# Row sums of reciprocals: a new hand-written order in which GpSimd squares most of the pairs and TensorE folds four rows

## The chip, the cores and the metric

The kernel runs on one core of a Trainium2 chip. The metric is the device time of one execution in microseconds (us). The core has five engines that run their own instruction lists side by side: TensorE (PE in the profile), VectorE (DVE), ScalarE (ACT), GpSimd (POOL) and SyncE (SP), which here issues every load and store. Sixteen DMA engines move the data.

## The reference

```python
x = abs(randn(32, 512, 1024)) + 1e-6      # float32
out = np.sum(1.0 / x, axis=-1)            # float32, shape (32, 512)
```

So 16384 rows of 1024 numbers are read, 67.1 MB, and one sum of reciprocals is written for each.

## The kernel before, in words

The 16384 rows are laid on 128 partitions with 128 rows each. What the kernel calls "row r" is therefore a 128x1024 tile, one row on each partition, 512 KB in memory. Rows 0 to 127 are loaded in order into a ring of 46 places (`ring`, `R = 46`), so row r lies in place r mod 46 and can be loaded only when everything that reads row r - 46 is done. The sums go to the 128 columns of `sums`, which is stored at the end.

No engine divides. A row is turned into sums of 1/x in one of two ways.

**Alone.** ScalarE replaces x by 1/sqrt(x) in place (token `A`, line 178; one instruction may take several neighbouring rows, written `A3+2`). Then the squares are summed, in one of four ways:

- `Z` (line 187): ScalarE squares the row and accumulates the sum.
- `G` (line 280), then `T` (line 283): GpSimd squares the row in place, VectorE adds it up.
- `Q` (line 240): VectorE multiplies the row by itself and accumulates, in one instruction with two inputs from the ring.
- `B` (line 255): VectorE takes batch-norm statistics of the two halves. The sums of squares lie in small tiles of counts, means and variances. Near the end of a block of such rows, `K` (line 265, ScalarE) squares the means and `M` (line 270, VectorE) adds them to the variances for all rows of the block at once. `C` is a plain square on ScalarE without a sum, for `T` to add.

**As a pair.** With a and b the two halves of a row, 1/a + 1/b = (a + b) / (a b). GpSimd multiplies the halves into one of five slots of `prod` (`P`, line 194). TensorE adds the halves in a bank of PSUM through an identity matrix (`U`, line 201, two matmuls). ScalarE takes 1/sqrt of the product in its slot (`L`) and squares it (`E`; both line 211). VectorE multiplies that by the sum in PSUM and accumulates (`R`, line 220). A pair row needs no `A`, and each of its later instructions works on 512 columns.

The order of all of this is one hand-written list, `PLAN`. Each engine executes its tokens in the order of the list, and a token waits only for the data it touches. `D` issues a load of so many rows from SyncE (line 170), `O` the stores of the finished columns (line 156); a last store of the remaining columns follows after the list. In the list before there are 25 loads: 2, 12, 12, 9 and 11 rows fill the ring, then 10, 8, 8, 8 and so on, down to four of one row. The last row, 127, comes as two halves (`PIECES`), which count as units 127 and 128. It ends:

```python
... A122 R119 A123 Q122 L121 Q123 A124 E121 Q124 A125
R121 A126 Q125 A127 A128 Q127 Z126 Q128
```

Of the kernel before, what the change touches and what calls it, by code (L numbers as in the profile page):

```python
# [11 lines left out]
def kernel(  # L12
# [17 lines left out]
    STATS = ((43, 3, 11), (80, 2, 18),)  # L30
    STORES = (0, 21, 43, 64, 81, 99, 116)
    S = float(2**17)
    FIT = 1.0 - 2.0**-17

    PLAN = """
        D2 D12 D12 D9 D11 A0+2 Z0 A2 A3 A4+3 G1+3 A7 A8 A9 G6+3 A10 T1 A11+3 T2+2 Z4 Z5 G9 Z10
        Z12 G11 T6+4 D10 A14 A15+2 G13 A17+3 G16 T11 T13 A20+4 G17 Q15 G19 T16+2 A24+2 G20 A26
        A27 G21 A28+2 G23+3 A30+2 T19+3 A32+3 Z14 D8 G26 C33 Z18 G27 Z22 Z29 G28 A35+2 G30+3
        T23+6 D8 A37+3 A40+4 G34+2 T30+2 A44+2 Z36 T32 G40 Z37 T33+3 D8 Z38 G44+2 U53@0 A46+2
        T40 A48 Q42 G47 A49 A50+3 B43 T44 P53@0 T45 A54+2 G50 B46 L53 T47 Z39 D6 B49 A56+6 T50
        B52 Q54 B55 A62+2 G57 Q56 E53 G60 Z41 D6 R53 Z48 T57 A64+6 B58 G62 T60 G63 B61 T62+2
        A70+2 G65+2 B64 Z51 D7 D6 B67 Z59 D5 G68+2 A72 T65+2 D4 A73+4 B70 G71+2 T68+2 D3 A77+2
        B73 A79 G78 T71+2 D2 K0 U81@1 A80 A82+2 G79 M0 B80 A84 U85@2 B82 P81@1 Z74 D2 T78+2 Z75
        G83 L81 Z76 D2 P85@2 B84 U89@3 A86+3 T83 P89@3 U91@4 P91@4 L85 B86 G87 L89 A90 B88 L91  # L50
        T87 E81 E85 E89 R81 E91 R85 Z77 D1 D1 D1 D1 D1 D1 R89 B90 A92+2 P95@0 U95@5 R91 A94 B92
        G93 L95 B94 A96 A97 T93 A98 B96 E95 B98 Z97 P99@1 U99@6 A100+2 R95 P103@2 L99 B100 G101
        A102 U103@7 L103 B102 A104 T101 E99 E103 R99 P107@3 U107@0 A105 R103 A106 B104 P109@4
        U109@1 L107 Q105 A108 L109 B106 E107 E109 R107 P111@0 U111@2 A110 B108 A112 P113@1 R109
        U113@3 L111 B110 L113 E111 B112 E113 P115@2 U115@4 A114 R111 P116@3 L115 R113 U116@5
        E115 B114 P118@4 A117 R115 U118@6 L116 K1 Q117 L118 E116 P119@0 M1 O0 A120 U119@7 R116
        E118 Q120 L119 E119 P121@1 U121@0 R118 A122 R119 A123 Q122 L121 Q123 A124 E121 Q124 A125
        R121 A126 Q125 A127 A128 Q127 Z126 Q128
# [3 lines left out]
    Square = mybir.ActivationFunctionType.Square  # L62
    mult = mybir.AluOpType.mult
    add = mybir.AluOpType.add
# [18 lines left out]
    ring = pool.tile([P, R, D], f32)  # L83
    sums = pool.tile([P, F], f32)
    prod = pool.tile([P, NP, H], f32)
    stat_rows = [i for lo, step, n in STATS for i in range(lo, lo + step * n, step)]
    stats = pool.tile([P, len(stat_rows), 2, 2, 3], f32)
# [9 lines left out]
    def place(u):  # L97
        return (u, 0, D) if u < NR else PIECES[u - NR]

    def area(u, n=1):  # L100
        r, at, w = place(u)
        if u >= NR:
            w, n = sum(place(i)[2] for i in range(u, u + n)), 1
        return ring[:, r % R : r % R + n, at : at + w]
# [35 lines left out]

    def rows(u, n=1):
        spaces = []
        for r, at, w in (place(i) for i in range(u, u + n)):
            spaces += [("row", r % R, i) for i in range(at, at + w, 128)]
        return spaces

    def half(u, at):
        return [("row", u % R, i) for i in range(at, at + H, 128)]

    loaded = 0  # L150
    summed = set()
    slot, bank = {}, {}
# [5 lines left out]
    with tc.manual_schedule():  # L158
        for _ in range(EARLY):
            nc.gpsimd.nop(hint="idle", nofuse=True)  # L160
        for op, u, n, b in (parse(tok) for tok in PLAN):
            if op == "D":
                n, u = u, loaded
                while n:
                    r, at, w = place(u)
                    m = min(n, R - r % R, NR - u, HALF - r % HALF) if u < NR else n
                    k = m
                    if u >= NR:
                        w, k = sum(place(i)[2] for i in range(u, u + m)), 1
                    inst = nc.sync.dma_start(  # L170
                        out=area(u, m),
                        in_=x_v[r // HALF, :, r % HALF : r % HALF + k, at : at + w],
                    )
                    note("SP", inst, writes=rows(u, m))
                    u, n = u + m, n - m
                loaded = u
# [8 lines left out]
            elif op == "Z":  # L185
                r = place(u)[0]
                inst = nc.scalar.activation(  # L187
                    out=area(u), in_=area(u), func=Square, accum_out=sums[:, r : r + 1]
                )
                summed.add(r)  # L190
                note("ACT", inst, writes=rows(u))
# [6 lines left out]
            elif op == "U":  # L198
                bank[u], r = b, u % R
                for h in range(2):  # L200
                    inst = nc.tensor.matmul(  # L201
                        ps[:, b],
                        lhsT=ident,
                        rhs=ring[:, r, h * H : (h + 1) * H],
                        start=h == 0,
                        stop=h == 1,
                    )
                    note("PE", inst, half(u, h * H), [("bank", b)])
            elif op in "LE":
# [8 lines left out]
            elif op == "R":  # L218
# [9 lines left out]
                    accum_out=sums[:, u : u + 1],  # L228
                )
                note("DVE", inst, [("bank", bank[u])], [("slot", slot[u])])  # L230
            elif op == "Q":
                r, at, w = place(u)
                joined = [u]
                while len(joined) < n:
                    joined += [i for i in range(NR, u) if place(i)[0] == r][-len(joined) :][:1]
                at -= sum(place(i)[2] for i in joined[1:])
                w += sum(place(i)[2] for i in joined[1:])
                row = ring[:, r % R, at : at + w]
                total = sums[:, r : r + 1]
                inst = nc.vector.tensor_tensor_reduce(  # L240
                    out=row,
                    in0=row,
                    in1=row,
                    scale=1.0,
                    scalar=total if r in summed else 0.0,
                    op0=mult,
                    op1=add,
                    accum_out=total,
                )
                summed.add(r)  # L250
                note("DVE", inst, writes=[s for i in joined for s in rows(i)])
            elif op == "B":
                i = stat_rows.index(u)
                for h in range(2):
                    inst = nc.vector.bn_stats(  # L255
                        out=stats[:, i, h], in_=ring[:, u % R, h * H : (h + 1) * H]
                    )
                    note("DVE", inst, reads=half(u, h * H), writes=[("stat", i)])
            elif op in "KM":
                lo, step, n = STATS[u]  # L260
                i = stat_rows.index(lo)
                part = stats[:, i : i + n]
                if op == "K":
                    mean = part[:, :, :, :, 1].rearrange("p f h e -> p (f h e)")
                    inst = nc.scalar.activation(  # L265
                        out=mean, in_=mean, func=Square, scale=float(H // 2) ** 0.5
                    )
                    engine = "ACT"
                else:
                    inst = nc.vector.tensor_reduce(  # L270
                        out=sums[:, lo : lo + step * (n - 1) + 1 : step],
                        in_=part[:, :, :, :, 1:].rearrange("p f h e k -> p f (h e) k"),
                        axis=mybir.AxisListType.XY,
                        op=add,
                    )
                    engine = "DVE"
                note(engine, inst, writes=[("stat", j) for j in range(i, i + n)])
            elif op == "G":
                row = area(u, n)
                inst = nc.gpsimd.tensor_tensor(out=row, in0=row, in1=row, op=mult)  # L280
                note("POOL", inst, writes=rows(u, n))
            elif op == "T":
                inst = nc.vector.tensor_reduce(  # L283
                    out=sums[:, u : u + n],
                    in_=area(u, n),
                    axis=mybir.AxisListType.X,
                    op=add,
                )
                note("DVE", inst, reads=rows(u, n))
# [34 lines left out]
```

## Time and profile before

| | |
|---|---|
| median of 3 runs | 166.06 us (166.04 to 166.06) |
| span of the profiled execution | 164.2 us; the runs count some 1.8 us more, which lie around the span |
| busy: ScalarE, VectorE, GpSimd | 145.7, 115.9, 108.8 us |
| busy: TensorE matmuls | 38.2 us |
| read from memory | 67.11 MB, 409 GB/s over the span |

The page has numbered parts: busy time of each engine, the span in 40 slices with a digit for each engine's busy share, the DMA queues, the chain of work that ended last, the costliest groups of instructions, and the DMA issues. "L178" is line 178 of the kernel. In a group, "mean ns" is the duration of one instruction; two instructions that follow each other on an engine can overlap at their ends, so the distance from one start to the next start is a little shorter. `SPq` is the queue in which SyncE issues DMAs.

### The profile page before, as it was taken

How to read it: one execution, taken by the hardware profiler on the slowest of the kernel's cores; microseconds unless marked ns; L12 is line 12 of the kernel's file. 1: busy time of each engine (PE TensorE's matmuls, PEld its weight loads, DVE VectorE, ACT ScalarE, POOL GpSimd, SP SyncE). 2: the span in 40 equal slices, each digit the busy share in tenths (PEclk: the TensorE clock that was granted, in tenths of full speed). 3: DMA queues.
4: the chain of work that ended last, by engine and by line, in shares of the span. 5: the costliest groups of instructions: out<-in, count | busy, mean ns of one | idle time of the engine just before them, and what ended most of it. 6: DMA issues, size and time to landing. Idle time of an engine off the chain costs nothing.

```text
span 164.2 us, 640 instructions
## 1 busy us (share of the span) xinstructions
PE 38.2 (23%) x68; PEld 14.4 (9%) x68; DVE 115.9 (71%) x147; ACT 145.7 (89%) x148; POOL 108.8 (66%) x56
## 2 busy tenths in 40 slices
PE   0000000000000000053000000065908198699700
PEld 0000000000000000020000000032302033234200
DVE  0000003559927039999999999999698969999894
ACT  3600199999999999999999999999999999999994
POOL 1000069998999999999507979999926195477300
PEclk9999999999999999999999999999975859999985
DMA  5999899899989899999998998999999999999970
GB/s 188 463 539 407 383 395 563 383 431 431 463 351 527 351 479 409 391 455 431 391 503 383 431 463 381 455 407 441 419 425 467 414 419 422 421 411 417 408 249 2
DMA packets 4611, 67.20 MB, mean 409 GB/s; under 512 B 1408, under 2 KB 1408, under 8 KB 2176
## 3 DMA queue, kind: packets, MB, share of 16 engines
q1 hardware_dynamic: 4608, 67.18, 96.3%
q14 instruction: 3, 0.02, 0.0%
HBM read 67.11 MB, written 0.07 MB: 409 GB/s over the span
## 4 chain that ended last, share of the span: by engine, by line
ACT 63%; DMA 26%; DVE 6%; issue 2%; POOL 2%; SPq 0%; DVEq 0%; POOLq 0%
ACT ring L178 47%; DMA ring<-in_x_dram 26%; ACT ring L187 10%; ACT prod L211 6%; DVE ring L240 2%; DVE stats L255 2%; POOL prod L194 2%; DVE prod L220 1%; DVE sums L283 0%; SPq L170 0%; ACT stats L265 0%; DVE sums L240 0%; DVE sums L220 0%; DVEq L240 0%; POOLq L194 0%
## 5 line engine op out<-in xcount | busy, mean ns | idle before, releaser
L178 ACT ACTIVATE ring<-ring 128x1024 f32<-128x1024 f32 (+4 forms) x65 | 104.1, 1658 | 15.2 <-DMA ring<-in_x_dram 15.1
L280 POOL TENSOR_TENSOR ring<-ring 128x1024 f32<-128x1024 f32 (+2 forms) x33 | 85.9, 2634 | 29.9 <-ACT ring L178 29.9
L283 DVE TENSOR_REDUCE sums<-ring 128x1 f32<-128x1024 f32 (+4 forms) x27 | 53.3, 1999 | 42.2 <-POOL ring L280 42.1
L201 PE MATMUL ps<-ring,ident 128*128 128x512 f32 x68 | 38.2, 712 | 117.2 <-DMA ring<-in_x_dram 115.9
L255 DVE BATCH_NORM_STATS2 stats<-ring 128x6 f32<-128x512 f32 x58 | 36.5, 679 | 3.1 <-ACT ring L178 3.1
L194 POOL TENSOR_TENSOR prod<-ring 128x512 f32<-128x512 f32 x17 | 22.5, 1339 | 15.0 <-DMA ring<-in_x_dram 10.8
L201 PEld LDWEIGHTS ps<-ring,ident 128*128 128x128 f32 x68 | 14.4, 224 | 140.2 <-POOL ring L280 71.6
L187 ACT ACTIVATE ring<-ring 128x1024 f32<-128x1024 f32 x23 | 23.9, 1041 | 0.0
L211 ACT ACTIVATE prod<-prod 128x512 f32<-128x512 f32 x34 | 19.8, 615 | 0.2
L240 DVE CUSTOM_DVE_ANT_0 ring<-ring 128x1024 f32<-128x1024 f32 (+1 forms) x12 | 17.6, 1480 | 0.5 <-ACT ring L178 0.4
L220 DVE CUSTOM_DVE_ANT_0 prod<-prod,ps 128x512 f32<-128x512 f32 x17 | 11.1, 676 | 0.1
L187 ACT ACTIVATION_READ_ACCUMULATOR ring<-ring 128x1 f32 x23 | 4.3, 187 | 0.0
L70 ACT ACT_TABLE_LOAD x1 | 1.3, 1283 | 0.7 <-PEq L308 0.7
L220 DVE DVE_READ_ACCUMULATOR2_ANT sums<- 128x1 f32 x17 | 1.4, 81 | 0.0
L240 DVE DVE_READ_ACCUMULATOR2_ANT sums<- 128x1 f32 x13 | 1.0, 81 | 0.0
L240 DVE CUSTOM_DVE_ANT_0 ring<-ring,sums 128x512 f32<-128x512 f32 x1 | 0.8, 752 | 0.1
masks.py:199 POOL TENSOR_SCALAR_AFFINE_SELECT ident<-ident 128x128 f32<-128x128 f32 x1 | 0.3, 293 | 0.5 <-POOL ident masks.py:197 0.5
L265 ACT ACTIVATE stats<-stats 128x44 f32<-128x44 f32 (+1 forms) x2 | 0.5, 272 | 0.0
L270 DVE TENSOR_REDUCE sums<-stats 128x11 f32<-128x88 f32 (+1 forms) x2 | 0.5, 264 | 0.0
masks.py:197 POOL MEMSET ident<- 128x128 f32 x1 | 0.2, 205 | 0.3 <-POOLq L308 0.3
L308 POOL MEMSET const-float32-0.0<- 128x1 f32 x1 | 0.1, 99 | 0.2 <-issue 0.2
L308 POOL MEMSET const-bfloat16-1.0<- 128x1 bf16 x1 | 0.1, 102 | 0.0
(2 smaller groups left out, 0.2 us busy)
## 6 DMA issues: line engine op xcount, KB each, us to landing
ring<-in_x_dram SPq DMA_DIRECT2D x2, 6144.0 KB, 25.8
ring<-in_x_dram SPq DMA_DIRECT2D x3, 4096.0 KB, 26.0
ring<-in_x_dram SPq DMA_DIRECT2D x3, 3072.0 KB, 26.3
ring<-in_x_dram SPq DMA_DIRECT2D x1, 5632.0 KB, 55.9
ring<-in_x_dram SPq DMA_DIRECT2D x1, 5120.0 KB, 32.4
ring<-in_x_dram SPq DMA_DIRECT2D x1, 4608.0 KB, 43.3
ring<-in_x_dram SPq DMA_DIRECT2D x4, 1024.0 KB, 37.8
ring<-in_x_dram SPq DMA_DIRECT2D x1, 3584.0 KB, 24.4
```

The lines of the kernel that those rows point to most:

```text
L70: nc.scalar.add_instruction(mybir.InstLoadActFuncSet(name=nc.get_next_instruction_name(), act_func_set_id=act_sets.index("abs_reciprocal_s ...
L178: inst = nc.scalar.activation(out=area(u, n), in_=area(u, n), func=Arsqrt if op == "A" else Square, scale=FIT if op == "A" else 1.0,)
L187: inst = nc.scalar.activation(out=area(u), in_=area(u), func=Square, accum_out=sums[:, r : r + 1])
L194: inst = nc.gpsimd.tensor_tensor(out=prod[:, b], in0=ring[:, r, :H], in1=ring[:, r, H:], op=mult)
L201: inst = nc.tensor.matmul(ps[:, b], lhsT=ident, rhs=ring[:, r, h * H : (h + 1) * H], start=h == 0, stop=h == 1,)
L211: inst = nc.scalar.activation(out=pair, in_=pair, func=Arsqrt if op == "L" else Square, scale=S * FIT if op == "L" else 1.0,)
L220: inst = nc.vector.tensor_tensor_reduce(out=pair, in0=pair, in1=ps[:, bank[u]], scale=S, scalar=0.0, op0=mult, op1=add, accum_out=sums[:, ...
L240: inst = nc.vector.tensor_tensor_reduce(out=row, in0=row, in1=row, scale=1.0, scalar=total if r in summed else 0.0, op0=mult, op1=add, acc ...
L255: inst = nc.vector.bn_stats(out=stats[:, i, h], in_=ring[:, u % R, h * H : (h + 1) * H])
L265: inst = nc.scalar.activation(out=mean, in_=mean, func=Square, scale=float(H // 2) ** 0.5)
L280: inst = nc.gpsimd.tensor_tensor(out=row, in0=row, in1=row, op=mult)
L283: inst = nc.vector.tensor_reduce(out=sums[:, u : u + n], in_=area(u, n), axis=mybir.AxisListType.X, op=add,)
```

## The change

The list is new, and so are some of its tokens.

- 18 of 21 pairs are now squared by GpSimd (`H`, in place in the slot) instead of by ScalarE (`E`, which stays for rows 39, 119 and 122). Before there were 17 pairs, all squared by ScalarE.
- Four rows (44, 45, 85, 86), after GpSimd has squared them, are folded by TensorE: `V44+2` adds the quarters of two rows into one PSUM bank by four matmuls, and `F44+2` on VectorE reduces the 2x256 columns there. This stands in for a `T` over two rows.
- `stats` now has a place for each of rows 0 to 121 and is zeroed by GpSimd at the start. Every sum of these rows, whatever made it, is written into one cell of it, and two `K`/`M` pairs (rows 0 to 77, rows 78 to 121) turn all of them into `sums`. Only rows 122 to 127 write `sums` themselves.
- Rows 125, 126 and 127 are counted in quarters of 256 columns (units 125 to 136). 23 loads bring everything: 17, 13 and 16 rows fill the ring, then 10, 8, 12, 9, 7, 7, 6, 5, 4, 3, 2, 2, 2, 1, 1 rows, rows 125 and 126, and row 127 as two quarters and a half.
- 13 idle instructions at the start of GpSimd's list are gone.
- By kinds, before and after: rows through `A` 111 and 107; `Z` 23 and 17; rows through `G` 46 and 31; rows through `T` 47 and 34; `B` 29 and 46; `Q` 13 and 6; `C` 1 row and 7; pairs 17 and 21.

```diff
-    EARLY = 13
...
-    PIECES = ((127, 0, 512), (127, 512, 512))
-    NR = 127
-    STATS = ((43, 3, 11), (80, 2, 18),)
-    STORES = (0, 21, 43, 64, 81, 99, 116)
+    NR = 125
+    C = D // 4
+    BLOCKS = (78, 122,)
+    STORES = (0, 9, 18, 27, 37, 46, 55, 64, 78)
...
+        D17 D13 D16 A8 A5+3 C5 A0+4 A14 G0 A4 Z1 G8 B4 A9+4 T5 G14 B7 T8 G2 A16 B12 Z11 G10
+        U26@0 T2 A29 T14 Z3 P27@0 B29 A23 G9 U27@1 A25 L27 T9+2 Z23 H27 A17+4 G16 T0 P26@1
+        B6 B25 D10 A21+2 G17 T16 A15 R27 C21 L26 C15 H26 A13 R26 T15 A24 C24 T21 A28 B19 G28
+        T17 A45 U34@2 A35+4 B20 P34@2 T24 P39@3 T28 G45 B13 A30+3 B18 G37 D8 B22 A40 A42+2
+        D12 G40 A41 T40 B41 A50 P51@4 U51@3 T37 A46 G43 L34 C42 U39@4 G31+2 C50 A44 T50 A47
+        T42+2 L51 H34 L39 E39 H51 C38 B30 G44 A52+4 T31 R51 U60@5 G36 B46 A48+2 P56@0 T36
+        V44+2@6 B35 P60@1 A57+2 B53 G49 A33 T38 G47 U56@7 Z54 T32 Z33 F44+2 R34 L60 D9 A61+3
...
+        P103@2 B97 L98 Z100 U98@4 H98 B99 A104 P102@3 U103@5 L101 Q104 L103 L102 R98 U101@6
+        A107+2 D4 P105@4 F85+2 B94 P106@0 U102@7 L105 B108 A109 H101 Z109 U105@0 B107 H102
+        L106 H103 R101 A110+3 D4 U113@1 B96 H105 R103 P113@1 U106@2 R102 Z110 B112 H106 D1
+        L113 U114@3 P114@2 R105 A115+2 B111 H113 R106 L114 D1 P118@3 U118@4 R113 A117 B115
+        H114 Z116 B117 A120 D2 O0 P119@4 U119@5 R114 L118 B120 L119 H118 E119 U122@6 A121
+        P122@0 R119 R118 K1 A123 Q121 L122 Q123 E122 A124 R122 A125+4 Q124 A129+4 Q125+4
+        A133+2 A135+2 Q129+4 Z133+4 M1
...
-        for _ in range(EARLY):
-            nc.gpsimd.nop(hint="idle", nofuse=True)
+        note("POOL", nc.gpsimd.memset(stats, 0.0), writes=result(0, BLOCKS[-1]))
...
+            elif op == "H":
+                pair = prod[:, slot[u]]
+                inst = nc.gpsimd.tensor_tensor(out=pair, in0=pair, in1=pair, op=mult)
+                note("POOL", inst, writes=[("slot", slot[u])])
+            elif op == "V":
+                bank[u] = b
+                w = H // n
+                for h in range(2 * n):
+                    inst = nc.tensor.matmul(
+                        ps[:, b].rearrange("p (n w) -> p n w", n=n),
+                        lhsT=ident,
+                        rhs=whole(u, n)[:, :, h * w : (h + 1) * w],
+                        start=h == 0,
+                        stop=h == 2 * n - 1,
+                    )
+                    note("PE", inst, rows(u, n), [("bank", b)])
+            elif op == "F":
+                inst = nc.vector.tensor_reduce(
+                    out=total(u, n),
+                    in_=ps[:, bank[u]].rearrange("p (n w) -> p n w", n=n),
+                    axis=mybir.AxisListType.X,
+                    op=add,
+                )
+                note("DVE", inst, [("bank", bank[u])], result(u, n))
```

More of the change, by code (lines that the diff above doesn't have):

```diff
@@ L275 @@
                     )
-                    engine = "DVE"
-                note(engine, inst, writes=[("stat", j) for j in range(i, i + n)])
+                    note("DVE", inst, means + result(lo, hi - lo))
             elif op == "G":
@@ L283 @@
                 inst = nc.vector.tensor_reduce(
-                    out=sums[:, u : u + n],
-                    in_=area(u, n),
+                    out=total(u, n),
+                    in_=whole(u, n),
                     axis=mybir.AxisListType.X,
```

141 lines of the change are left out of this document (68 added, 73 removed).

## The prediction

> **What bounds the kernel now.** I read the page from its head to the chain of work that ended last.
>
> ```profile
> span 164.2 us, 640 instructions
> ...
> ACT  3600199999999999999999999999999999999994
> ...
> q1 hardware_dynamic: 4608, 67.18, 96.3%
> q14 instruction: 3, 0.02, 0.0%
> ...
> ACT 63%; DMA 26%; DVE 6%; issue 2%; POOL 2%; SPq 0%; DVEq 0%; POOLq 0%
> ```
>
> Two things are full at once. The load queue's packets fill 96.3% of the span, 158.1 of 164.2 us, so 128 rows cost 1.235 us each and the stream hardly pauses. ScalarE is at 9 in every slice from about 20 us to the end. So two views matter next: when the stream ends (the table by stages), and what stands behind it (the timelines of ScalarE and VectorE at the end).
>
> ```profile
> 140.00:150.00 10.00, 8.69 (x21) 3.51 (x20) 10.00 (x23) 9.87 (x15) 6.26 (x5) 1.00 1.00 420
> ...
> 159.00:160.00 1.00, 0.00 (x0) 0.00 (x0) 1.00 (x3) 1.00 (x2) 0.00 (x0) 0.50 0.21 24
> ```
> ```profile
> 157.79 3.03 ACT L178 ACTIVATE ring<-ring 128x1024 f32<-128x1024 f32 x4
> 160.73 1.04 ACT L187 ACTIVATE ring<-ring 128x1024 f32<-128x1024 f32 x1
> 161.67 0.19 ACT L187 ACTIVATION_READ_ACCUMULATOR ring<-ring 128x1 f32 x1
> ```
> ```profile
> 161.18 0.75 DVE L240 CUSTOM_DVE_ANT_0 ring<-ring,sums 128x512 f32<-128x512 f32 x1
> 161.85 0.08 DVE L240 DVE_READ_ACCUMULATOR2_ANT sums<- 128x1 f32 x1
> ```
>
> The last columns are DMA share and GB/s, ahead of them come PE, PEld, DVE, ACT and POOL. From 140 to 150 us the DMA share is 1.00 with DVE and ACT full too. Between 159 and 160 us the stream runs out: a share of 0.21, 24 GB/s. ScalarE ends at 161.86, VectorE at 161.93, some 2 us behind the last data; the last store and the end take the remaining 2.3 us to 164.2. The runs shown (median 166.06) lie 1.8 us above that span; I carry both 2.3 and 1.8 over unchanged.
>
> So a faster kernel must shorten either the stream or what ScalarE and VectorE still have to do when the last rows arrive. ScalarE work saved in the middle is worth nothing by itself.
>
> **Part 1: what is removed, added and moved, by engine.** Durations, busy and mean ns:
>
> ```profile
> L255 DVE BATCH_NORM_STATS2 stats<-ring 128x6 f32<-128x512 f32 x58 | 36.5, 679 | 3.1 <-ACT ring L178 3.1
> L178 ACT ACTIVATE ring<-ring 128x1024 f32<-128x1024 f32 x36 | 36.4, 1041 | 11.6 <-DMA ring<-in_x_dram 11.6
> L178 ACT ACTIVATE ring<-ring 128x2048 f32<-128x2048 f32 x15 | 28.3, 1895 | 3.6 <-DMA ring<-in_x_dram 3.5
> L187 ACT ACTIVATE ring<-ring 128x1024 f32<-128x1024 f32 x23 | 23.9, 1041 | 0.0
> L194 POOL TENSOR_TENSOR prod<-ring 128x512 f32<-128x512 f32 x17 | 22.5, 1339 | 15.0 <-DMA ring<-in_x_dram 10.8 <-DVE stats L255 2.4 <-DVE sums L283 1.7
> L280 POOL TENSOR_TENSOR ring<-ring 128x3072 f32<-128x3072 f32 x4 | 21.2, 5306 | 20.3 <-ACT ring L178 20.3
> L211 ACT ACTIVATE prod<-prod 128x512 f32<-128x512 f32 x34 | 19.8, 615 | 0.2
> L178 ACT ACTIVATE ring<-ring 128x3072 f32<-128x3072 f32 x7 | 19.2, 2747 | 0.0
> L283 DVE TENSOR_REDUCE sums<-ring 128x1 f32<-128x1024 f32 x15 | 17.9, 1206 | 27.4 <-POOL ring L280 27.4
> L280 POOL TENSOR_TENSOR ring<-ring 128x2048 f32<-128x2048 f32 x5 | 17.9, 3601 | 0.9 <-ACT ring L178 0.9
> L220 DVE CUSTOM_DVE_ANT_0 prod<-prod,ps 128x512 f32<-128x512 f32 x17 | 11.1, 676 | 0.1
> L270 DVE TENSOR_REDUCE sums<-stats 128x18 f32<-128x144 f32 x1 | 0.3, 293 | 0.0
> L270 DVE TENSOR_REDUCE sums<-stats 128x11 f32<-128x88 f32 x1 | 0.2, 235 | 0.0
> ```
> ```profile
> 155.81 0.61 ACT L211 ACTIVATE prod<-prod 128x512 f32<-128x512 f32 x1
> 156.33 1.04 ACT L178 ACTIVATE ring<-ring 128x1024 f32<-128x1024 f32 x1
> 157.27 0.61 ACT L211 ACTIVATE prod<-prod 128x512 f32<-128x512 f32 x1
> ```
> ```profile
> 156.14 1.22 DVE L240 CUSTOM_DVE_ANT_0 ring<-ring 128x1024 f32<-128x1024 f32 x1
> ```
> ```profile
> 5.48 1.91 ACT L178 ACTIVATE ring<-ring 128x2048 f32<-128x2048 f32 x1 [3.46 <-DMA ring<-in_x_dram]
> ```
>
> Starts show what one costs in a full queue: a 512-column activation 0.52 us, a row 0.945; two and three rows in one instruction 1.80 and 2.65 (their means less the same 0.095); a `Z` 1.04 (0.945 and the read of its sum). VectorE by the same reduction (0.07 to 0.08): a `B` row 1.20, `R` 0.605, `T` 1.12, a `Q` near the end 1.15.
>
> - ScalarE: `L` and `E` fall from 34 to 24 (-5.2 us), `Z` from 23 to 17 (-6.2), rows through `A` from 111 to 107 (-3.4 at 0.85 for a row inside a larger instruction), `C` adds 6 (+5.4). Together some -9.5 us. But its work now begins with the first load of 17 rows, near 24 us (3 us to the first bytes and 17 rows) instead of 5.5 us for two rows and 20 us for the rest. It gains room in the middle only.
> - VectorE: 17 more `B` rows (+20.4), 13 fewer rows through `T` (about -14.5), 7 fewer `Q` (about -8.5), 4 more `R` (+2.4), 2 `F` over 512 PSUM columns (taken at an `R`, 0.6 each): about +1.
> - GpSimd: 15 fewer rows through `G` (-26 at 1.7), 4 more `P` (+5.4), 18 `H` (below) and the memset. No row shows a memset of this size; it lies under the first load, which covers it for over 20 us, so I take nothing for it, between a gain of nothing (the 13 idle instructions ran there too) and a delay that only these 20 us would use up.
> - TensorE: 16 more matmuls, none that an engine on the path waits for.
>
> **H has no row.** It is a square of 512 columns in place. The nearest rows are `G`, the same form on 2048 columns (3.60 us for two rows, 5.31 for three, so 1.71 for one more row), and `P`, 512 columns with two different inputs. `G`'s slope carries 512 columns to 0.85 plus a fixed 0.19: 1.04 us. Ends: 0.85 (slope alone) and 1.34 (`P`'s mean). I take 1.04, because `H` has the form of `G`: one operand, read twice, written in place.
> The Trainium skill (GPSIMD Engine Reference, section 3.1) gives a two-input elementwise operation about 2.6 cycles an element at 1.2 GHz; by that 512 columns are an estimated 1.1 us beside the fixed part, and `H` would cost what `P` does. `P`'s row agrees with it; `G`'s 1.71 us for 1024 columns is 2.0 cycles and does not. What the higher price does is the first rival.
>
> **Part 2: does the stream still run dry nowhere?** A load waits in SyncE's queue until its places are free.
>
> ```profile
> ring<-in_x_dram SPq DMA_DIRECT2D x1, 5120.0 KB, 32.4
> ```
> ```profile
> L170 SPq EVENT_SEMAPHORE  x18: 17/17/28, 39.0 to 148.3; - x18
> ```
> ```profile
> 150.95 1.29 POOL L194 TENSOR_TENSOR prod<-ring 128x512 f32<-128x512 f32 x1 [1.20 <-DMA ring<-in_x_dram]
> 153.44 1.29 POOL L194 TENSOR_TENSOR prod<-ring 128x512 f32<-128x512 f32 x1 [1.20 <-DMA ring<-in_x_dram]
> ```
>
> The first waiting load (10 rows, issued at 39.0) lands 32.4 us later: row 55 is there at 71.4. GpSimd's waits at the end put row 122 at about 153.3. Between lie 67 rows at 1.22 us. With the same stream the new loads land at 81 (row 63), 96 (75), 107 (84), 115, 124, 131, 137.2 (row 109), 142 (113), 146, 148.4, 150.8 and 153.3 us. Adding up each engine's queue from its first row, the load of rows 46 to 55 is free to go at about 49 us (`B6`), rows 56 to 63 at 64 (`B13`), rows 64 to 75 at 67 (`B22`), rows 76 to 84 at 90.4 (`Z33` on ScalarE, `T32` on VectorE at 89.7), rows 92 to 98 at 105 (`B52`), the rest over 10 us early. They are needed at 59, 71, 81, 96 and 115. The smallest lead is 5.5 us, of which some 2 us go from issue to first bytes (the first load's 2 rows are 2.4 us of stream and are waited for until 5.5 us, after an issue at about 1). So the stream stays whole. Two loads fewer are worth little: 2-row loads land 2.49 apart, 1.245 a row against 1.222, 0.05 us for each load. Quarter rows cost about that again. I take no change, between 0.5 us either way; the last data are there by 160.0.
>
> **Part 3: the end.** ScalarE is level with the stream at row 109. From 137.2 us its queue holds, by the list: eight single `A` (7.56), two of two rows (3.60), one of three (2.65), two halves (1.04), four `Z` (4.16), seven `L` and two `E` (4.68), `K1` on 176 columns (0.25). That is 23.94. Five instructions directly follow the one that made their input (`Z109`, `Z110`, `E119`, `E122`, `Z133+4`) and lose the overlap; what that costs stands in the chain of before:
>
> ```profile
> 153.35 0.02 issue
> 153.38 0.63 ACT prod L211
> ```
>
> Here `E` follows its own `L`: 0.63 instead of 0.52 and 0.02 of issue, 0.13 us; five make 0.65. With 0.1 for the last read the sum is 24.7: ScalarE ends at 161.9. The last half row is needed at 160.1 and has landed by then, so it adds nothing.
>
> VectorE starts at 139.05 (after `A107+2`): eight `B` rows (9.6), ten `R` (6.05), five `Q` at 1.15 (5.75), `M1` over 352 cells (0.51, on the line through 235 ns for 88 and 293 ns for 144), and about 0.9 of waits for `A110`, `E119` and `A124`: 22.8, ending at 161.85. GpSimd has seven `P` and eight `H` after 137.2 and waits for rows 113, 116, 118 and 120 on the way, with 0.3 us to spare at `P119`; `L119` stands behind it.
>
> Both ends are level with 161.86 and 161.93 of before. **Sum: 0.0 us**, span 164.2, time 166.0.
>
> **The rivals.**
>
> 1. *GpSimd becomes the bound (slower).* Seven `H` stand in GpSimd's queue ahead of `P119`. Above 1.10 us each, the 0.3 us are used up and ScalarE waits at `L119`, with `E119` and all the rest behind it. At `P`'s price, 0.25 more, seven cost 1.75 - 0.3 = 1.4 us: 167.4. For: GpSimd's list is tight there. Against: `G`'s slope. 0.12.
> 2. *Waits add up (slower).* VectorE has no slack from 139 us on and ScalarE none from 137; a late `R` delays `B120` and `K1`. Some ten handovers at 0.05 to 0.1: 0.4 to 1.0 us, about 166.7. 0.14.
> 3. *The stream runs dry (slower).* Rows 76 to 84 are freed last. If VectorE is over 3.5 us late at `T32`, the stream stops for the rest; priced at 1 us: 167.0. Against: VectorE has waits before 90 us that absorb delay. 0.07.
> 4. *The stream comes earlier (faster).* The page's second queue, three instruction fetches, uses the same DMA engines, and a load lands with its slowest engine. Fewer loads and other fetches could bring rows 109 to 122 some 0.5 us sooner, and ScalarE's queue with them: 165.5. 0.27.
> By the Trainium skill (DMA: Bandwidth & Descriptors, section on the anatomy of one DMA), each DMA has about 2 us of fixed cost; two fewer would be an estimated 4 us. The 0.05 us between landings does not bear that out here, since loads queue behind each other.
> 5. *The change does not do what it says:* ScalarE's saved 9.5 us return as waiting for rows. That is inside my forecast.
>
> **How the numbers follow.** Forecast, ends level, 0.40: 166.0, its own range 165.75 to 166.35. About 0.2% (0.33 us) is what a measurement of this kernel can tell from no change. Faster is rival 4 and a little of the forecast, 0.29; within 0.2% most of the forecast and a part of 2, 0.40; slower the rest of 2, with 1 and 3, 0.31. The range reaches from rival 4 with a little more (165.2) to rival 1 (167.4).
>
> **What would show it.** Right: DMA share 1.0 until 158 us; ScalarE waiting for DMA several times before 137 us and hardly after; both ends at about 161.9; `H` near 1.04 us. Wrong: an idle time of ScalarE ahead of line 250 released by GpSimd (rival 1); DMA share below 0.9 between 90 and 110 us (rival 3); ScalarE's last read ending before 161.5 (rival 4).

## The result, and the profile after

The changed kernel takes 166.36 us (median of 13 runs, 166.22 to 166.73), the kernel before 166.08 us (13 runs on the same chip, 165.94 to 166.32). The ratio is 1.0019 [1.0011, 1.0027]: 0.28 us slower. In the profiled executions the span (from the first instruction to the last) goes from 164.24 to 164.45 us, 0.21 us more. The profiled execution of the changed kernel took 166.23 us, the second shortest of its 13; what lies around the span comes under "Open".

From the page of the changed kernel come the span, the busy times, ScalarE's 40 slices, the queues and the chain that ended last:

```profile
span 164.4 us, 693 instructions
...
PE 60.4 (37%) x100; PEld 23.8 (14%) x100; DVE 116.2 (71%) x182; ACT 137.0 (83%) x126; POOL 103.6 (63%) x74
...
ACT  3000019999999999979999999999999999999994
...
q1 hardware_dynamic: 4736, 67.18, 96.2%
q14 instruction: 5, 0.03, 0.0%
...
DMA 47%; ACT 45%; DVE 4%; POOL 2%; issue 1%; SPq 0%; ACTq 0%
```

ScalarE is busy for 137.0 us in place of 145.7, and the end has not moved with it. Its row of slices says why: the 9s begin at the seventh slice, some 4 us later than before (24.15 against 19.97 us), with zeros in place of the two early rows. The load queue is as full as it was, 158.2 us of packets in 164.4.

The view of waits says the same in one line for each kernel (us in total, times, longest). First the kernel before, then the changed one:

```profile
ACT ring L178 <- DMA ring<-in_x_dram: 15.1, 3, 11.4
```
```profile
ACT ring L188 <- DMA ring<-in_x_dram: 24.0, 4, 22.1
```

**8.7 us less work, 8.9 us more waiting for rows.** ScalarE's timeline of the changed kernel shows where it waits (the bracket is the idle time ahead of the instruction and what ended it), and its last two instructions:

```profile
24.15 10.19 ACT L188 ACTIVATE ring<-ring 128x1024 f32<-128x1024 f32 x6 [22.13 <-DMA ring<-in_x_dram]
59.24 10.91 ACT L188 ACTIVATE ring<-ring 128x1024 f32<-128x1024 f32 x6 [0.33 <-DMA ring<-in_x_dram]
71.36 2.00 ACT L188 ACTIVATE ring<-ring 128x1024 f32<-128x1024 f32 x2 [1.22 <-DMA ring<-in_x_dram]
131.20 1.91 ACT L188 ACTIVATE ring<-ring 128x2048 f32<-128x2048 f32 x1 [0.32 <-DMA ring<-in_x_dram]
...
137.29 1.91 ACT L188 ACTIVATE ring<-ring 128x2048 f32<-128x2048 f32 x1
...
161.01 1.06 ACT L197 ACTIVATE ring<-ring 128x1024 f32<-128x1024 f32 x1
161.97 0.19 ACT L197 ACTIVATION_READ_ACCUMULATOR ring<-ring 128x1 f32 x1
```

Behind the first 17 rows it waits 1.9 us in all, and after 131 us never more than 0.12 us (ahead of 137.29). ScalarE's busy time from 71.36 us to the end shows where the saved work lay (length of the stretch, busy time and instructions, then TensorE's granted clock, DMA share and GB/s). First the kernel before, then the changed one:

```profile
71.36:164.20 92.84, 90.01 (x101) 0.92 0.95 401
```
```profile
71.36:164.20 92.84, 90.16 (x89) 0.74 0.95 401
```

Behind 71 us ScalarE has 0.15 us more to do than before. All that the change saves on it lies ahead of 71 us, where rows are still to come, and there it turns into waiting. Its last read ends at 162.16 us, 161.86 before. VectorE's end, and the table by stages at the end (DMA share and GB/s last):

```profile
161.52 0.51 DVE L300 TENSOR_REDUCE sums<-stats 128x44 f32<-128x352 f32 x1
```
```profile
137.00:158.00 21.00, 17.43 (x40) 7.05 (x38) 20.53 (x47) 20.76 (x27) 16.82 (x15) 1.00 1.01 415
158.00:159.00 1.00, 0.00 (x0) 0.00 (x0) 0.92 (x1) 1.00 (x3) 0.00 (x0) 0.51 0.91 245
159.00:160.00 1.00, 0.00 (x0) 0.00 (x0) 1.00 (x3) 1.00 (x2) 0.00 (x0) 0.50 0.39 38
160.00:161.00 1.00, 0.00 (x0) 0.00 (x0) 1.00 (x3) 0.97 (x2) 0.00 (x0) 0.50 0.10 5
```

VectorE ends at 162.03 (161.93 before). The stream runs at full share to 158 us, and the last packet of a row ends at 159.32 us (159.24 before). A load has landed when all sixteen DMA engines have reported it: for the last half row fifteen have by 159.77, the sixteenth at 160.28 us (159.91 before). The 5 GB/s between 160 and 161 us are stores of finished columns. The `A` of the last half row starts at 160.36. So three things end together: ScalarE's queue, VectorE's queue, and the last half row with the 1.8 us of work that hang on it. The last store is issued at 162.18 (162.00 before) and takes 1.43 us (1.41 before), and so the span is 0.21 us longer.

The groups that the change touches (busy, mean ns; then idle time before them):

```profile
L203 POOL TENSOR_TENSOR prod<-ring 128x512 f32<-128x512 f32 x21 | 26.6, 1276 | 9.4 <-DMA ring<-in_x_dram 9.3
L220 POOL TENSOR_TENSOR prod<-prod 128x512 f32<-128x512 f32 x18 | 18.6, 1039 | 4.8 <-ACT prod L250 4.8
...
L235 DVE TENSOR_REDUCE stats<-ps 128x2 f32<-128x512 f32 x2 | 1.4, 682 | 0.0
L175 POOL MEMSET stats<- 128x1464 f32 x1 | 1.3, 1323 | 0.0
```

`H` costs 1.039 us. The memset of 1.3 us lies under the first load. In the span, 8 KB instruction fetches sit at 76.54, 83.59, 111.87 and 159.51 us; the kernel before has three, at 65.78, 100.21 and 112.13.

### The profile page after: what moved, and what is told of

Its sections match the earlier page's. It is cut to its first block, busy times and chain, and to the rows that moved or that the text cites. A ratio compares the mean times of both kernels' runs of the same rounds, so it can differ in the third digit from the quotient of the medians.

```text
span 164.4 us, 693 instructions
## 1 busy us (share of the span) xinstructions
PE 60.4 (37%) x100; PEld 23.8 (14%) x100; DVE 116.2 (71%) x182; ACT 137.0 (83%) x126; POOL 103.6 (63%) x74
## 4 chain that ended last, share of the span: by engine, by line
DMA 47%; ACT 45%; DVE 4%; POOL 2%; issue 1%; SPq 0%; ACTq 0%
DMA ring<-in_x_dram 47%; ACT ring L188 32%; ACT ring L197 7%; ACT prod L250 5%; DVE stats L312 2%; DVE stats L285 1%; POOL ring L309 1%; POOL prod L220 1%; SPq L181 0%; ACT stats L295 0%; ACTq L348 0%
## 5 line engine op out<-in xcount | busy, mean ns | idle before, releaser
L188 ACT ACTIVATE ring<-ring 128x1024 f32<-128x1024 f32 (+6 forms) x65 | 106.2, 1686 | 24.2 <-DMA ring<-in_x_dram 24.0
L285 DVE BATCH_NORM_STATS2 stats<-ring 128x6 f32<-128x512 f32 x92 | 57.4, 681 | 35.8 <-ACT ring L188 35.8
L309 POOL TENSOR_TENSOR ring<-ring 128x1024 f32<-128x1024 f32 (+1 forms) x28 | 57.7, 2076 | 36.6 <-ACT ring L188 36.6
L210 PE MATMUL ps<-ring,ident 128*128 128x512 f32 x84 | 50.3, 754 | 78.5 <-POOL ring L309 40.0
L312 DVE TENSOR_REDUCE stats<-ring 128x1 f32<-128x1024 f32 (+1 forms) x32 | 40.1, 1276 | 7.0 <-POOL ring L309 4.1
L210 PEld LDWEIGHTS ps<-ring,ident 128*128 128x128 f32 x84 | 19.4, 241 | 107.5 <-issue 62.5
L220 POOL TENSOR_TENSOR prod<-prod 128x512 f32<-128x512 f32 x18 | 18.6, 1039 | 4.8 <-ACT prod L250 4.8
L197 ACT ACTIVATE ring<-ring 128x1024 f32<-128x1024 f32 x17 | 17.8, 1045 | 0.1
L226 PE MATMUL ps<-ring,ident 128*128 128x512 f32 x16 | 10.7, 832 | 16.4 <-POOL ring L309 16.4
L250 ACT ACTIVATE prod<-prod 128x512 f32<-128x512 f32 x24 | 14.3, 616 | 0.1
L226 PEld LDWEIGHTS ps<-ring,ident 128*128 128x128 f32 x16 | 4.5, 286 | 23.2 <-POOL ring L309 17.7
L272 DVE CUSTOM_DVE_ANT_0 ring<-ring 128x1024 f32<-128x1024 f32 x6 | 7.3, 1256 | 0.1
```

The costliest lines, as they stand in the source:

```text
L188: inst = nc.scalar.activation(out=area(u, n), in_=area(u, n), func=Arsqrt if op == "A" else Square, scale=FIT if op == "A" else 1.0,)
L197: inst = nc.scalar.activation(out=area(u, n), in_=area(u, n), func=Square, accum_out=column)
L210: inst = nc.tensor.matmul(ps[:, b], lhsT=ident, rhs=ring[:, r, h * H : (h + 1) * H], start=h == 0, stop=h == 1,)
L220: inst = nc.gpsimd.tensor_tensor(out=pair, in0=pair, in1=pair, op=mult)
L226: inst = nc.tensor.matmul(ps[:, b].rearrange("p (n w) -> p n w", n=n), lhsT=ident, rhs=whole(u, n)[:, :, h * w : (h + 1) * w], start=h == ...
L250: inst = nc.scalar.activation(out=pair, in_=pair, func=Arsqrt if op == "L" else Square, scale=S * FIT if op == "L" else 1.0,)
```

## The experiments

After the result three explanations stood. **Theory 1**: ScalarE's own queue is late, by the five pauses in it. **Theory 2**: three chains end level, so that shortening one brings next to nothing. **Theory 3**: VectorE's longer list brings a fourth instruction fetch, which holds up the last rows and with them the end. Times below are medians, ratios are to the kernel before on the same chip (166.14 to 166.15).

**The same kernel once more.**

> The changed kernel once more, on the chip of the following three, as their yardstick and for a second profile. Expected: 166.2 to 166.5 us, ScalarE ending near 162.15, and the fetch of 8 KB at about 159.5 us again if it hangs on VectorE's instruction count (theory 3); elsewhere or absent if it is chance.

Measured: 166.38 us (12 runs, 166.12 to 167.04), ratio 1.0015 [1.0005, 1.0025]. The fetch is at 159.46 us again, ScalarE ends at 162.18, VectorE at 162.03, span 164.46. The result is repeatable, and so is where it ends.

**ScalarE without four of its five pauses.** Between an instruction and the one that uses its output another one is put (for that ScalarE squares the pair 118 and GpSimd the pair 119, the other way round than before); the pause ahead of the last `Z133+4` stays:

```diff
- A109 H101 Z109 U105@0 B107 H102 L106 H103 R101 A110+3
+ A109 H101 L106 Z109 U105@0 B107 H102 H103 R101 A110 A111+2
...
- L119 H118 E119 U122@6 A121 P122@0 R119 R118
+ L119 E118 H119 U122@6 A121 P122@0 R118 R119
...
- E122 A124 R122 A125+4 Q124
+ A124 E122 A125+4 Q124 R122
```

> The changed kernel with ScalarE's order altered after row 109, so that four of its five stalls behind a producer go: L106 ahead of Z109, A110+3 as A110 and A111+2, E118 and H119 in place of E119 and H118, A124 ahead of E122. Theory 1 (ScalarE's queue alone sets the end): 0.45 us of stalls go, ScalarE ends at 161.7 instead of 162.16 and the time falls by 0.4 us to about 165.95. Theory 2 (three chains are level: ScalarE 162.16, VectorE 162.03, and the last half row, which landed at 160.28 and has 1.8 us of ScalarE work behind it): the gain is 0.05 to 0.15 us, because ScalarE then waits for the last half row, ending at about 162.1.

Measured: 166.34 us (11 runs), ratio 1.0016 [1.0007, 1.0024]. ScalarE's timeline at the end of this kernel:

```profile
157.58 2.51 ACT L188 ACTIVATE ring<-ring 128x1024 f32<-128x1024 f32 x3
160.33 0.63 ACT L188 ACTIVATE ring<-ring 128x512 f32<-128x512 f32 x1 [0.24 <-DMA ring<-in_x_dram]
160.99 1.06 ACT L197 ACTIVATE ring<-ring 128x1024 f32<-128x1024 f32 x1
161.96 0.19 ACT L197 ACTIVATION_READ_ACCUMULATOR ring<-ring 128x1 f32 x1
```

The chain that ended last, in order of time, now leads through the load:

```profile
150.84 9.47 DMA ring<-in_x_dram
160.31 0.02 issue
160.33 0.64 ACT ring L188
160.97 0.02 issue
160.99 1.06 ACT ring L197
```

The four pauses are gone, ScalarE is early, and waits 0.24 us for the last half row; it ends 0.01 us earlier than in the changed kernel, VectorE 0.02. The 0.4 us of theory 1 do not come. Against theory 1, for theory 2: the chains are level.

**Fewer instructions on VectorE.** Ten pairs of `T` over neighbouring rows become one instruction each (`T8+3`, `T14+2`, `T16+2` and so on to `T90+2`), alone and together with the order above.

```diff
- T49 ... T50
+ T49+2
...
- T64 ... T65
+ T64+2
```

> The changed kernel with ten pairs of neighbouring reductions on VectorE merged into one instruction each (for example T31 and T32 into T31+2), all before 130 us, so that VectorE has ten instructions fewer. Theory 3 (the fourth instruction fetch, at 159.51 us, comes when VectorE's list passes its 192nd instruction, and delays the last half row from about 159.8 to 160.28): the page counts 4 instead of 5 packets of the instruction queue, the last data come 0.3 to 0.5 us earlier. Theory 2: even so the time stays within 0.1 us of 166.36, because ScalarE's queue (162.16) is not shortened. If the stream's end alone set the end, the time would fall by 0.35 us.

> Both edits at once: ScalarE's four stalls gone and ten VectorE instructions fewer. Theory 2 and 3: now all three chains are shorter, ScalarE ends at about 161.8, VectorE at about 161.85, and the time falls by 0.25 to 0.35 us to about 166.05, more than the sum of what each edit brings alone. Theory 1: the same 0.4 us as the first edit alone.

Measured: 166.74 us (5 runs), ratio 1.0036 [1.0024, 1.0049], and 166.68 us (5 runs), ratio 1.0035 [1.0021, 1.0049]. Both missed what was expected: the last half row of the first kernel lands later, at 160.87 us, and the second kernel is slower than the changed one, not 0.3 us faster. The fourth fetch moves behind the engines' end, to 166.51 and 165.42 us. A merged `T` comes where its second row is due, and a load that waits for the first row's place goes later. SyncE's timeline of the first of the two kernels has the loads that went at 65.11 and 90.48 us in the changed kernel:

```profile
67.34 0.33 SPq L181 DMA_DIRECT2D ring<-in_x_dram  x1
91.98 0.80 SPq L181 DMA_DIRECT2D ring<-in_x_dram  x2
```

That looks like the reason why its rows land some 0.4 us later from row 63 on (81.84 us in place of 81.33) and ScalarE ends at 162.79. It is not: the second kernel issues the same load as late, at 67.24 us, and row 63 is there at 81.31. What differs is the spread of the sixteen DMA engines in that load, 1.62 us between the first and the last to finish in the first kernel, 0.98 in the second, 1.06 in the changed one: in the first, one engine is further behind. An 8 KB fetch at 80.48 us that falls on the engine which is last anyway would do that; which engine took it the trace doesn't name. There is one fetch more, too, on another queue. The page's part 3 for this kernel:

```profile
q1 hardware_dynamic: 4736, 67.18, 95.9%
q8 instruction: 1, 0.02, 0.0%
q14 instruction: 3, 0.02, 0.0%
```

It is one packet of 16 KB at 154.92 us, 1.1 us long, and the load that it meets is complete at 157.07; with the 0.4 us it would have been 156.3. The second kernel's profiled execution has no such packet and is the shortest of its five runs (166.22): ScalarE ends at 161.78, the last half row lands at 159.86, VectorE ends at 162.0, span 164.32. With ScalarE and the last half row both earlier, VectorE is the third of the level chains, as theory 2 has it. Why its other four runs lie at 166.63 to 166.78 no trace here shows.

**One load more.** The first load of 17 rows is split into 2 and 15 (`D17` becomes `D2 D15`), the rest is left alone, so that ScalarE still begins with row 8 of the second load.

> The changed kernel with its first load of 17 rows split into 2 and 15 rows; rows 5 to 14 still come first in ScalarE's list, so ScalarE still starts with row 8 when the second load is there. This tests only what one more load costs the stream. By the 0.05 to 0.07 us that loads queued behind each other showed: 0.0 to 0.1 us more, within what can be told from no change. If every load cost about 2 us of its own: 2 us more.

Measured: 166.62 us (11 runs, 166.24 to 167.34), ratio 1.0031 [1.002, 1.0042]. The profiled execution has the 16 KB packet again (154.40 us, 1.085 us), a span of 164.7 and ScalarE's end at 162.26. One load more does not cost 2 us: ahead of that packet every load lands 0.1 to 0.4 us earlier than in the changed kernel (row 122 at 153.21 in place of 153.33 us). The median is 0.24 us above that of the same kernel once more; the delay that the packet brings is one candidate.

**Five merges only**, those that no load waits for closely (`T49+2`, `T61+2`, `T64+2`, `T77+2`, `T90+2`; one load still goes at 106.05 in place of 105.01 us and lands within 0.1 us of before), alone and with the order without pauses.

> The changed kernel with only five pairs of reductions on VectorE merged (rows 49 and 50, 61 and 62, 64 and 65, 77 and 78, 90 and 91), none of which a load waits for within 10 us: the earlier edit of ten merges also held back the loads of rows 56 to 63 and 76 to 84 by 2 us. Theory 3: VectorE's list passes its 192nd instruction only at its last ones, the fetch falls behind 161 us or off the end, and the last half row lands at about 159.8 instead of 160.28. Theory 2 (three level chains): the time stays within 0.1 us of the changed kernel, since ScalarE's queue still ends at 162.15. If the stream's end alone set the end: 0.35 us less.

> The five safe merges and the removal of ScalarE's four stalls together. Theory 2: now ScalarE ends at about 161.8, the last half row at 159.8 allows 161.65, and VectorE, at 162.0, is what remains: 0.1 to 0.2 us less than the changed kernel. Theory 1 (ScalarE's queue alone): 0.4 us less.

The first missed: 167.34 us (6 runs), ratio 1.0077 [1.0062, 1.0092], a whole microsecond. The engines end nearly as in the changed kernel (ScalarE 162.25, VectorE 162.12), so the time is behind them. In the waits of SyncE's queue, the end waits for the last store. This kernel, then the changed one:

```profile
SPq L348 <- DMA out_dram<-sums: 1.9, 1, 1.9
```
```profile
SPq L348 <- DMA out_dram<-sums: 0.8, 1, 0.8
```

The DMA view from 162.0 to 165.6 us of the kernel with five merges (GB/s in 40 slices of 0.09 us, packets by queue, the store's time to landing):

```profile
GB/s 0 0 0 0 0 0 0 0 0 0 0 0 64 149 145 0 0 0 0 0 7 11 0 0 0 0 0 0 0 0 0 0 0 0 0 0 0 0 0 0
...
q1 hardware_dynamic: 144, 0.03, 3.7%
q14 instruction: 1, 0.01, 1.0%
...
out_dram<-sums SPq DMA_DIRECT2D x1, 25.0 KB, 2.5
```

The store takes 2.5 us from issue to landing in place of 1.4. The fourth fetch has moved to 163.29 us, into the store: fifteen DMA engines are done by 163.71, and the last packets of the sixteenth share start at 163.87, where the fetch ends (the 7 and 11 behind the gap), and land at 164.80. The second kernel: 166.30 us (12 runs), ratio 1.0014 [1.0003, 1.0026]. With this order the fourth fetch stays at 159.52 us, and yet the last half row lands at 159.91, as in the kernel before. ScalarE ends at 161.78, VectorE at 161.98, and the store goes at 162.04: VectorE alone now sets the end. The spans of its 12 runs average 164.41 us, those of the kernel before 164.38 and those of the changed kernel 164.46: the lateness inside the span is all but gone, and the median is still 0.15 us above the kernel before. It has the lowest median of the versions tried, and it is no better than the kernel before.

**The fetch by itself, in the kernel before.** Idle instructions at the start of VectorE's list lengthen it without work: 29 to bring the fourth fetch to where the changed kernel has it, 22 to bring it into the last store.

```diff
+ for _ in range(29):
+     nc.vector.nop(hint="idle", nofuse=True)
```

> The kernel before, with 29 idle instructions put at the start of VectorE's list and nothing else. VectorE has nothing to do until 27 us, so they cost it no time, but its list now passes its 192nd instruction at about 158.5 us. Theory 3: a fourth fetch of 8 KB appears there and the last half row lands 0.3 to 0.5 us later than 159.91; ScalarE was 0.25 us late for it, so the time rises by 0.1 to 0.25 us, which is about what the change cost. If fetches do not matter: no change from 166.1 us.

> The kernel before with 22 idle instructions at the start of VectorE's list, 7 fewer than in the earlier run. The changed kernel with five VectorE instructions fewer took 1.0 us more although its engines ended as before: its fetch of 8 KB lay at 163.3 us, while the last store was in flight, which took 2.5 us instead of 1.4. If that is the cause, 22 idle instructions bring the fetch of this kernel to 163 us too, the last store takes about 2.5 us, and the time is about 167.1 though no work is added; with 29 it was 166.2. If the merged reductions themselves cost that 1 us: 166.2 again.

Measured: 166.20 us (11 runs), ratio 1.0002 [0.9993, 1.001], and 166.12 us (11 runs), 1.0000 [0.9991, 1.0009]. The fetches appear, at 159.71 and 163.18 us. With the first, the last half row lands at 160.34 in place of 159.91, some 0.15 us of it a stream that is later as a whole (the half row ahead of it lands at 159.22 in place of 159.07); ScalarE ends at 162.04 and VectorE at 162.10, and the runs hardly move. So theory 3 has the place of the fetch right, and its price wrong: a fetch there costs this kernel at most some 0.17 us (the upper end of the interval), and does not explain the 0.28 us. The second missed its expectation of a microsecond. The DMA view of that kernel from 162.0 to 164.5 us:

```profile
GB/s 0 0 0 0 0 0 0 0 0 0 0 0 0 0 27 41 27 4 131 0 0 0 0 0 0 0 0 0 0 0 0 0 0 0 0 0 0 0 0 0
...
q14 instruction: 1, 0.01, 1.2%
...
out_dram<-sums SPq DMA_DIRECT2D x1, 6.0 KB, 1.4
```

Here the store's packets (27 41 27 4) are through a tenth of a microsecond ahead of the fetch (131), and the store takes its 1.4 us. That store is also smaller, 6 KB where the changed kernel's has 25. The window in which a fetch costs a microsecond is narrow, and the delayed store stands shown in one kernel's trace only.

**Is ScalarE work in the middle worth nothing?** Nine half squares go back from GpSimd to ScalarE (`H` to `E`, 0.52 us each): the first nine (rows 26 to 83), the same nine with a first load of 4 rows, so that ScalarE starts at 8 us, and the last nine (rows 98 to 118). **Theory A** holds that ScalarE's queue is full from its first row on, so that they come back at the end nearly whole; the prediction's sentence holds that early ones cost nothing; and by **C** it is the late start that sets the end.

```diff
- T9+2 Z23 H27 A17+4
+ T9+2 Z23 E27 A17+4
```

> The changed kernel with the first nine of its eighteen GpSimd squares (rows 26, 27, 34, 51, 56, 60, 69, 82, 83; all before row 98) given back to ScalarE as E. Theory A (ScalarE is full from the landing of row 50 at 71 us to the end; its waits for DMA after that add up to 0.3 us): two of the nine vanish in the waits at 59 and 71 us, seven cost 0.52 each and one 0.13 more as it follows its own L, 3.8 - 0.3 = 3.4 us: about 169.8. Theory B (what I wrote in the prediction: work saved on ScalarE in the middle is worth nothing by itself): within 0.3 us of 166.4.

> The same nine squares on ScalarE, and ScalarE started earlier: the first load of 17 rows is split into 4 and 13 rows, and A0+4 and Z1 come first, 4.5 us of work that now lies before 24 us. Theory C (the GpSimd squares pay for the later start of ScalarE): about 166.5, the 3.4 us come back. Theory A: the time won early is lost again in the waits for rows 45 and 50 at 59 and 71 us, so the kernel stays at about 169.8.

> The changed kernel with the last nine GpSimd squares (rows 98, 101, 102, 103, 105, 106, 113, 114, 118) given back to ScalarE. ScalarE gets nine times 0.52 us more after 131 us, where it never waits for more than 0.1 us: 4.5 to 4.9 us more, about 171.0. If GpSimd (tight by 0.3 us at its product for row 119) had been a bound of the end, part of that would come back: under 4 us.

Measured, with 4 runs each: early nine 170.01 us, ratio 1.0231 [1.0214, 1.0247]; with the early start 169.98 us, 1.0236 [1.0221, 1.025]; late nine 170.59 us, 1.0274 [1.0257, 1.0291]. ScalarE ends at 165.71, 165.10 and 166.19 us, VectorE in the first two 0.30 us behind it. The waits of ScalarE, one line for each of the three kernels:

```profile
ACT ring L188 <- DMA ring<-in_x_dram: 22.9, 2, 22.3
```
```profile
ACT ring L188 <- DMA ring<-in_x_dram: 21.8, 5, 10.9
```
```profile
ACT ring L188 <- DMA ring<-in_x_dram: 23.9, 4, 22.2
```

Nine early halves use up the waits at 59 and 131 us and half of that at 71 us, 1.3 us in all, and move ScalarE's end by 3.55 us; seven of the nine run behind 71 us. Nine late ones move it by 4.03: of their 4.68 us some 0.4 come back because the new squares stand in three of the five pauses, and 0.25 fill waits for rows at 131 and 137 us. An early start of 4 rows is lost again in waits for rows at 23.7 and 39.5 us (10.85 and 3.55 us) and at 71 us (1.21), and the time stays, so C falls. Theory A holds: behind the first 17 rows ScalarE has no more to give than the 1.9 us that it waits at 59, 71 and 131 us.

## Why the prediction was right and wrong

**Right: the mechanism.** The saved ScalarE work returns as waiting for rows (8.7 us and 8.9 us), the stream stays whole, both queues decide the end, and they end level with the last rows. The forecast of 166.0 missed by 0.36 us; 166.36 lies inside the whole range and 0.01 us outside the range of the forecast alone.

**Right in the main: the terms of Part 1.** ScalarE's saving came out at 8.7 us for some 9.5, 0.5 of the difference because the two `K` take 1.0 us in place of 0.5 and stand in no term. `H` took 1.039 us (1.04 taken), far from `P`'s 1.276. The Trainium skill (GPSIMD Engine Reference, section 3.1), by which `H` would have cost what `P` does, is contradicted by this row: squaring a slot in place took 0.24 us less than multiplying two halves into another tile. `F` took 0.68 for 0.6, the memset hid under the first load, and GpSimd became no bound: its last waits are for rows and for ScalarE, and it is not waited for at the end. Rival 1 fell.

**Right: Part 2.** SyncE's timeline of the changed kernel has the loads that wait for places:

```profile
65.11 0.33 SPq L181 DMA_DIRECT2D ring<-in_x_dram  x1
67.49 0.33 SPq L181 DMA_DIRECT2D ring<-in_x_dram  x1
90.48 0.80 SPq L181 DMA_DIRECT2D ring<-in_x_dram  x2
105.01 1.28 SPq L181 DMA_DIRECT2D ring<-in_x_dram  x3
```

The prediction had 64, 67, 90.4 and 105. The share of DMA is 0.99 to 1.01 in every stage from 24 to 158 us, and row 109 was there at 137.27 (137.2 said). Rival 3 fell. So did rival 2: behind 137 us VectorE's listed waits are 0.21 and 0.19 us, where some 0.9 was taken, and ScalarE waits for no other engine. Rival 4, an earlier stream, fell too: two loads fewer brought no row sooner.

**Wrong: Part 3, "Sum: 0.0 us".** That is the step that failed, by the size of two terms. The first is ScalarE's queue from row 109 on. It was put at 24.7 us; it took 24.87, from 137.29 to 162.16, and it began 0.09 later than said. So it ended 0.26 us behind the 161.9 of the prediction and 0.30 behind the kernel before. In the timeline of the changed kernel `K1` on 176 columns stands ahead of the next `A` like this:

```profile
154.54 0.43 ACT L295 ACTIVATE stats<-stats 128x176 f32<-128x176 f32 x1
154.87 1.04 ACT L188 ACTIVATE ring<-ring 128x1024 f32<-128x1024 f32 x1
```

It costs 0.33 us from start to start and not 0.25. The prediction names no row for that 0.25; the two `K` of the kernel before, on 44 and 72 columns, took 0.246 and 0.298 us, and a line through them gives 0.49 for 176 columns, of which the next instruction overlaps some 0.1. The five pauses cost 0.14 to 0.15 us each with the longer instruction behind them, 0.72 together for 0.65, and `A107+2` took 0.02 more. VectorE started `B108` at 139.4, not 139.05, because its own list was full rather than waiting for `A107+2`, and needed 22.6 us for the rest, not 22.8: 0.18 us late in sum.

The second term is the 1.8 us around the span, which the prediction carries over unchanged without a reason. The 13 runs of the changed kernel have 1.90 us there on average. So 162.16, 2.29 to the end of the span and 1.90 around it make 166.35; the prediction added up 161.9, 2.3 and 1.8. These errors of 0.1 to 0.3 us are small beside 164, but the forecast of no change was a difference of two ends, and they are all that it missed by. What lengthens the time around the span stays open.

**Wrong: "The last half row is needed at 160.1 and has landed by then, so it adds nothing."** It was there at 160.28, 0.08 us before its `A` started. It did not set the end, but left no room for a better ScalarE: that is why taking away four pauses moved ScalarE's end by only 0.01 us.

**Wrong: "ScalarE work saved in the middle is worth nothing by itself."** Saved work was worth nothing here because all of it lay ahead of 71 us, where ScalarE can only wait longer for rows; behind that, it had as much to do as before. With this list, the nine half squares given back early, seven of them behind 71 us, cost 0.4 us of their 0.52 each at the end. The sentence should have said: what is saved is worth the wait that it does not turn into.

**Open.** What makes up the 0.28 us is shown only in part. For the kernel run once more the record has every run's span beside its time, for it and for the kernel before on the same chip. The span of the changed kernel averages 164.46 us against 164.38 before, 0.08 more, and the time around it 1.96 us against 1.79, 0.17 more. In 64 runs of the kernel before, and 22 with idle instructions, the time around the span is never over 1.85 us; in 15 of the 25 runs of the changed kernel it is 1.89 to 2.54. So the larger part lies where no trace reaches. The profiled execution has 1.78 there, and its 0.21 us of longer span is more than the average shows.

The longest runs (up to 166.73 and 167.04, against 166.32 and 166.43 of the kernel before beside them) are of both kinds: 166.73 has a span of 165.0, 167.04 one of 164.5. The 16 KB fetch seen near 155 us in two profiles delayed a load by some 0.8 us there, and runs with it could make the first kind. In four other profiles, the changed kernel's among them, it comes just behind the span, at 164.9 to 165.7 us, and in none of the kernel before; but there the time around the span is 1.78 to 1.95 us, and 2.0 in the repeat's profile without it. This is argued, not shown.

## What to carry to other kernels

When an engine's busy time falls and the end does not, compare its total wait by releaser before and after: here 8.7 us of work became 8.9 us of waiting for the first load. Where several queues end within 0.2 us of each other, a forecast of "no change" needs every term of each queue to hundredths, small instructions included, and an edit that shortens one of them is worth only the distance to the next. What lies around the span is a term too, and was not the same for two kernels of one task (1.79 and 1.90 to 1.96 us). Code length counts as well: where instruction fetches fall among the loads and stores changes with the edits of a list, one such place cost a microsecond here, and an edit's time should be read with their places at hand.

## What the runs showed of the hardware

- Instruction fetches share the DMA engines with the data. A packet of 8 KB takes 0.31 to 0.63 us in these traces, and a load or store has landed only with its last engine; in front of the last store it cost 1.1 us (2.5 in place of 1.4). The fourth fetch depends on the length of VectorE's list: it comes near 159.5 us in the changed kernel, appears in the kernel before when 22 or 29 idle instructions are added, and moves to 163.3 and 166.5 us as five and ten instructions are taken away. When it comes, 190 or 191 of VectorE's instructions, waits included, have begun in seven of these traces. It is not their number alone: with five taken away and the order without pauses it stays at 159.5, with 187 begun. The lists of other engines count too: with the nine squares moved from GpSimd to ScalarE, the third fetch goes from 111.9 to between 141 and 147 us, and the fourth comes near 161 us with 184 or 185 begun. The Trainium skill (Runtime: NRT & Kernel Launch, section on instruction fetch mechanics) speaks of blocks of 16 KiB that are fetched out of sight; the packets here are of 8 and 16 KB, and their delay is to be seen.
- An activation that reads what the one before it wrote starts 0.12 to 0.13 us later than an independent one: `Z109` 1.08 us after the start of `A109`, where independent rows follow each other by 0.945.
- A load issued at 67.2 us in place of 65.1, with some 4 us of earlier rows still to come, lost nothing: its 8 rows were complete at 81.31 and 81.33 us. In another kernel, with 67.3 us, they were complete at 81.84.
